# An encoder block with retention and windowed attention: attention's other work dealt out by K steps, values in a place of their own, sums and decays of the setup moved

## The chip, the cores and the metric

The kernel runs on one core of a Trainium2 chip. The metric is the device time of one execution in microseconds (us), and of several executions the median is taken. All engines of the core (TensorE for matmuls, VectorE, ScalarE, GpSimd, and SyncE, which issues transfers) run at the same time and wait for each other by semaphores. A row of the profile names them PE (with PEld for the load of weights into it), DVE, ACT, POOL and SP.

## The reference

One layer of a bidirectional encoder over 1024 positions and 16 learned meta tokens, with a width of 1024, in 32-bit floating point:

```python
u = _rms_norm(h, pre_w)
z = u @ w_in                      # q, k, v, gates of both branches
...
o_r = _bidirectional_retention(rq, rk, rv, lg_f, lg_b)[:, META_PAD:]   # 4 heads, decays exp(i * log_sigmoid(dec))
...
y_r = o_r.astype(h.dtype) @ w_rb
...
o_a = _windowed_sink_attention(aq, ak, av, sink)[:, META_PAD:].reshape(B, T, ATT_Q)   # 8 heads, 2 groups
o_a = o_a * jax.nn.silu(ag.astype(jnp.float32))
y_a = o_a.astype(h.dtype) @ w_ab
mix = jax.nn.sigmoid(gr) * y_r + jax.nn.sigmoid(ga) * y_a
out = mix @ w_o
return h + _rms_norm(out, post_w)
```

Retention is computed in chunks of 128 positions, forward and backward with decays of their own. Attention takes blocks of 128 queries against the block before, the same block, the block after and the 16 meta keys.

## The kernel before

**Numbers in two parts.** Each 32-bit operand is given to TensorE as two operands of the type fp32r: a high part (a copy into that type, by ScalarE or, in `pool_hi`, by GpSimd) and a low part (operand minus high part, by VectorE in `dve_lo`, L77). A product is three matmuls, high by high, low by high and high by low (`mm3`, L69 to L71). One step over 128 of the 1024 input channels is called a K step; a whole projection of a tile, `proj`, has eight K steps, 24 matmuls.

**Setup (to about 42 us).** `x` comes in eight slices `xr0` to `xr7`. For each, ScalarE makes the high part and VectorE the low part (L317), TensorE runs one K step of retention's first query and key projections for all tiles (`qk0_mm`), ScalarE squares the slice, and a running sum of squares is kept (`add_square`, L306; the first sum is on GpSimd, the others on VectorE). The weights of the first query and key come in parts (`w0_part`). The decays are a chain of small operations on VectorE (`decays`, `decay_series`, `decay_exponents`, L192 to L211), with powers on GpSimd (L214, L269). After that `pack_meta` copies the meta columns into `xm` (L128, four casts), the first values' weights `wv0` are split (one low half on VectorE, L77, one on GpSimd, L102), and the projections `pv0_0`, `pv0_1` and so on follow. The rope rotation of a projection (`rope_evac`, L161 to L164) is three operations of VectorE that read the PSUM bank, and an addition on GpSimd.

**Retention (to about 347 us).** Four heads; beside each head's scans a generator supplies projections of the next. `fill()` takes the next item of a generator, here one whole projection. At the end of a head the output is normalized (L584), transposed (L552) and scaled (L557), and stored to DRAM by SyncE.

**Attention (about 347 to 597 us).** Four head pairs of eight query blocks. For a block, `stage1` splits the query (GpSimd L74, VectorE L77), makes the scores of both heads in the two PSUM banks of `p2`, adds the mask and takes the row maximum on VectorE (L1202), takes the exponential on ScalarE (L1204), and scales on GpSimd (L1216). `stage2` transposes the result (L1226 to L1233) and splits it again (`pah`, `pal`, `pbh`, `pbl`). `stage3` multiplies it with the values. The values are projected by `gen_av` (nine groups, `pav`) into `vraw`, which lies in the pool `ap`; that pool opens when retention's pool is closed. Beside `gen_av` runs `sums_of_x`: SyncE loads slices of x again (L661), ScalarE scales them (L666), VectorE takes four differences of each (L668), and SyncE stores them (L672). `FILL_A` names the blocks after which a projection is traced: of the same head pair's second half, of the next head pair, in head pair 2 of the second group of keys, and in head pair 3 of gates 6 and 5 (`gen_gate`).

**Output (to the end).** Blocked matrix products of both branches and of the output, one long run of matmuls.

**What sets the order.** Each engine works in an order that is fixed when the kernel is built. A scheduler with a model of the time picks it: what is traced earlier has priority, and what waits can be overtaken by something else that is ready. `tc.issue_after(p)` pins: what is traced inside stands behind instruction `p` in the order. Buffers of a tag, and PSUM banks (three `pj`, two `p1`, two `p2`, one `p3`), are given out in turn.

Of the kernel before, what the change touches and what calls it, by code (L numbers as in the profile page):

```python
# [14 lines left out]
NM = 16  # L15
# [10 lines left out]
FILL_A = (0, 1, 3, 4, 5, 6)  # L26
# [12 lines left out]
def block_kernel(ctx: ExitStack, tc: tile.TileContext, xT, x, w_in, w_rb, w_ab, w_out, vecs, dec, sink,  # L39
# [50 lines left out]
    def load_w(src, u, act=False):  # L90
        hi, lo = [], []
        for s in range(2):
# [8 lines left out]
            if act and s:  # L101
                nc.gpsimd.tensor_tensor(l, raw, h.bitcast(F32), ALU.subtract)  # L102
            else:
                dve_lo(l, raw, h)
# [84 lines left out]
    def decays():  # L189
# [6 lines left out]
        return v.tensor_scalar(acc, ss, 1.0 / 17, None, op0=ALU.mult).ins  # L196
# [20 lines left out]

    def decay_table(hs):
        for h in hs:
# [3 lines left out]
            nc.scalar.activation(t, t, AF.Exp)  # L223
            nc.vector.tensor_scalar(DT[:, h], t, SCALE, None, op0=ALU.mult)
# [17 lines left out]
    with tc.tile_pool(name="setup", bufs=1, reuse_waits="tile") as st:  # L242
# [24 lines left out]
        exponentials()  # L267
        with tc.issue_after(raised[0]):
            nc.gpsimd.tensor_tensor(e, ecst[:, 0:8], na, ALU.pow)  # L269
# [18 lines left out]
        for i in range(6):  # L288
# [16 lines left out]
        def add_square(k):  # L305
            sums[k] = (nc.vector if k > 1 else nc.gpsimd).tensor_tensor(squares[k], squares[k - 1], squares[k], ALU.add).ins  # L306

        for k in range(KT):
            t = xr[k]
            if k == 1:  # L310
                with tc.issue_after(head):
                    series = decays()
            parts = [(0, 528), (528, T)] if k == 0 else [(0, T)]
            for a, b in parts:
                nc.scalar.activation(xh[k][:, a:b], t[:, a:b], AF.Copy, scale=vec[:, k:k + 1])
                with tc.issue_after(sums[k - 2]) if k > 3 else tc.issue_after(series) if k == 1 else ExitStack():
                    low = nc.vector.scalar_tensor_tensor(xl[k][:, a:b], t[:, a:b], vec[:, k:k + 1],  # L317
                                                         xh[k][:, a:b].bitcast(F32), op0=ALU.mult, op1=ALU.subtract)
                if not a:
                    head = low.ins  # L320
            if k == 1:
# [4 lines left out]
                decay_columns()  # L326
            if k == 3:
                fifth()
# [3 lines left out]
            if k > 1:  # L332
                with tc.issue_after(low.ins), tc.issue_after(exponents):
# [19 lines left out]
        with tc.issue_after(split):  # L353
            evac_qk0(0)
# [53 lines left out]

    r_stack = ExitStack()
    rp = r_stack.enter_context(tc.tile_pool(name="rp", bufs=1, reuse_waits="tile"))  # L410

    def gen_qk(h):
# [3 lines left out]
        for i, (a, b) in enumerate(PIECES):  # L416
            t = proj(w, P, a, b, f"pk{h}_{i}")
            rope_evac(t, a, b, kt[:, i], f"k{h}_{i}")
            yield
        for i, (a, b) in enumerate(HALVES):  # L420
            t = proj(w, 0, a, b, f"pq{h}_{i}")
# [7 lines left out]
    def retention(h, fill):  # L429
# [133 lines left out]
        for c in range(NB, 0, -1):  # L563
# [54 lines left out]
    def gen_aq(hp, i):  # L618
# [4 lines left out]
        for e_ in range(2):  # L623
            t = proj(wq[hp], P * e_, a, b, f"paq{hp}_{i}{e_}")
# [8 lines left out]
    def gen_ak(g):  # L633
# [4 lines left out]
        for i, (a, b) in enumerate(PIECES):  # L638
            t = proj(wak[0], P * g, a, b, f"pak{g}_{i}")
# [777 lines left out]
```

## Time and profile before

| | us |
|---|---|
| median of 3 runs (lowest, highest) | 1098.11 (1097.82, 1101.93) |
| the profiled execution's own time | 1098.95 |
| its span, first to last instruction | 1097.2 |
| around the span | 1.75 |
| TensorE busy | 1072.2 (98%) |
| VectorE busy | 877.4 (80%) |
| ScalarE busy | 488.4 (45%) |
| GpSimd busy | 247.9 (23%) |
| mean granted clock of TensorE | 0.99 |

The profile shows one execution. Rows of a timeline give the start, the length, the engine, the line, the operation, what is written and read, the shapes, and how many in a row; in square brackets stands how long the engine had been idle before and what ended that. Grouped rows end with the busy time of the group, the mean of one in nanoseconds, and the idle time before them. The granted clock is the share of TensorE's full clock that the throttle allowed.

### The profile page before, as it was taken

The numbers are of one execution on the slowest core, as the hardware profiler recorded it, in microseconds if no ns is written. First come the engines' busy times: TensorE is split into PE (matmuls) and PEld (weight loads), VectorE is DVE, ScalarE is ACT, GpSimd is POOL, SyncE is SP. The second block draws the span as 40 slices with busy tenths as digits, with TensorE's granted clock in tenths as the row PEclk, the third lists the DMA queues.
The fourth block names the chain that finished last, engine by engine and source line by source line (L and its number), as shares of the span: only waits on it lengthen the run. The fifth ranks groups of instructions, "written<-read, shape, count | busy, mean of one in ns | idle before, by whom it ended". The sixth has DMA issues, their size and how long they took to land.

```text
span 1097.2 us, 17244 instructions
## 1 busy us (share of the span) xinstructions
PE 1072.2 (98%) x5973; PEld 925.4 (84%) x5973; DVE 877.4 (80%) x1868; ACT 488.4 (45%) x1132; POOL 247.9 (23%) x350
## 2 busy tenths in 40 slices
PE   8899999999998999999999999999999999999996
PEld 7899999998988988988887878888888788787885
DVE  7887778877957888988667876888889889867765
ACT  7141432513414454445667544454456446433442
POOL 5434324233322434455220000000000000110032
PEclk9899999998999999999999999999999999999999
DMA  7121111111115961121114763779874755789463
GB/s 287 39 77 38 42 40 58 59 40 39 59 40 183 321 225 49 40 77 58 50 49 154 251 208 124 247 229 349 275 272 129 228 199 199 233 201 330 121 115 78
DMA packets 75800, 159.46 MB, mean 145 GB/s; under 512 B 8128, under 2 KB 19904, under 8 KB 74944
## 3 DMA queue, kind: packets, MB, share of 16 engines
q1 hardware_dynamic: 71824, 151.78, 40.2%
q0 software_dynamic: 3456, 6.29, 3.8%
q8 instruction: 47, 0.77, 0.3%
q14 instruction: 41, 0.34, 0.1%
q10 hardware_dynamic: 432, 0.28, 0.1%
HBM read 105.89 MB, written 52.43 MB: 144 GB/s over the span
## 4 chain that ended last, share of the span: by engine, by line
PE 88%; DMA 5%; DVE 4%; ACT 1%; issue 1%; SPq 0%; POOL 0%; DVEq 0%; POOLq 0%; ACTq 0%
PE bz L70 6%; PE bz L69 6%; PE bz L71 6%; PE pv L69 3%; PE pv L70 3%; PE pv L71 3%; PE paq L70 3%; PE paq L71 3%; PE paq L69 3%; PE br L70 2%; PE bo L70 2%; PE bo L69 2%; PE bo L71 2%; PE br L69 2%; PE br L71 2%; PE ba L70 2%
## 5 line engine op out<-in xcount | busy, mean ns | idle before, releaser
L1051 POOL DMA_DIRECT2D mx_d<-c1a x4 | 3.7, 922 | 398.3 <-DVE c1a L1042 398.3
L70 PE MATMUL bz<-big,llz 128*128 128x512 f32 x208 | 82.4, 396 | 0.4 <-DVE llz L77 0.4
L71 PE MATMUL bz<-big,lhz 128*128 128x512 f32 x208 | 81.7, 394 | 0.0
L69 PE MATMUL bz<-big,lhz 128*128 128x512 f32 x208 | 81.2, 396 | 0.3 <-ACT lhz L772 0.3
L69 PE MATMUL pv<-wh,big 128*128 128x256 f32 x256 | 74.5, 291 | 0.0
L70 PE MATMUL pv<-wh,big 128*128 128x256 f32 x256 | 73.6, 287 | 0.0
L71 PE MATMUL pv<-wl,big 128*128 128x256 f32 x256 | 73.6, 287 | 0.0
L69 PE MATMUL bz<-T,lhz 128*128 128x512 f32 x156 | 61.7, 395 | 0.0
L70 PE MATMUL bz<-T,llz 128*128 128x512 f32 x156 | 61.5, 395 | 0.0
L71 PE MATMUL bz<-T,lhz 128*128 128x512 f32 x156 | 61.3, 394 | 0.0
L1204 ACT ACTIVATE p<-p,nm 128x400 f32<-128x400 f32 (+1 forms) x64 | 38.5, 602 | 35.3 <-DVE nm L1202 32.5
L1216 POOL TENSOR_SCALAR p<-p,den 128x400 f32<-128x400 f32 (+1 forms) x60 | 36.1, 612 | 71.0 <-DVE den L1210 44.5
L70 PE MATMUL paq<-big,wl 128*128 128x512 f32 x128 | 51.2, 400 | 0.0
L69 PE MATMUL paq<-big,wh 128*128 128x512 f32 x128 | 51.0, 398 | 0.0
L71 PE MATMUL paq<-big,wh 128*128 128x512 f32 x128 | 50.9, 397 | 0.0
L69 PEld LDWEIGHTS pv<-wh,big 128*128 128x128 f32 x256 | 49.5, 193 | 0.6 <-DVE vl L77 0.4
L70 PEld LDWEIGHTS pv<-wh,big 128*128 128x128 f32 x256 | 49.5, 193 | 0.1
L71 PEld LDWEIGHTS pv<-wl,big 128*128 128x128 f32 x256 | 49.3, 193 | 0.0
L77 DVE TENSOR_TENSOR wl<-wr,wh 128x1024 fp32r<-128x1024 f32 x33 | 46.1, 1400 | 3.2 <-POOL wh L74 3.1
L69 PEld LDWEIGHTS bz<-big,lhz 128*128 128x128 f32 x208 | 39.0, 188 | 10.4 <-ACT lhz L772 1.3
L70 PEld LDWEIGHTS bz<-big,llz 128*128 128x128 f32 x208 | 39.1, 188 | 9.7 <-DVE llz L77 0.6
L71 PEld LDWEIGHTS bz<-big,lhz 128*128 128x128 f32 x208 | 39.1, 188 | 9.0
(618 smaller groups left out, 3666.4 us busy)
## 6 DMA issues: line engine op xcount, KB each, us to landing
wr<-in_w_in_dram SPq DMA_DIRECT2D x35, 512.0 KB, 3.6
wrz<-in_w_in_dram SPq DMA_DIRECT2D x28, 512.0 KB, 5.4
tg<-tg_d SPq DMA_DIRECT2D x32, 256.0 KB, 4.9
T<-preT SPq DMA_DIRECT2D x6, 1024.0 KB, 8.0
oTr_d<-ost SPq DMA_DIRECT2D x16, 256.0 KB, 2.1
xs<-in_xT_dram SPq DMA_DIRECT2D x16, 256.0 KB, 5.0
xsT<-xs SPq DMA_DIRECT2D x16, 256.0 KB, 5.3
oTa_d<-oa SPq DMA_DIRECT2D x16, 256.0 KB, 2.2
```

Of the source, the lines that this page charges most:

```text
L69: nc.tensor.matmul(o, ah, bh, start=first, stop=False, **kw)
L70: nc.tensor.matmul(o, al, bh, start=False, stop=False, **kw)
L71: return nc.tensor.matmul(o, ah, bl, start=False, stop=last, **kw).ins
L77: return nc.vector.tensor_tensor(o, i, hi.bitcast(F32), ALU.subtract).ins
L1051: nc.gpsimd.dma_start(d, to, accum_op=ALU.add)
L1204: nc.scalar.activation(p[:, 0:wid], p[:, 0:wid], AF.Exp, scale=-1.0, bias=nm_[:, e_:e_ + 1], accum_out=den[:, e_:e_ + 1])
L1216: nc.gpsimd.tensor_scalar(pt[e_][:, 0:wid], pt[e_][:, 0:wid], den[:, e_:e_ + 1], 1.0, op0=ALU.mult, op1=ALU.mult)
```

## The change

The tables for dealing out work, and the generators: `proj` gives the control back after each K step but the last, so an item of a generator is now one K step (three matmuls). Retention asks for `fill(KT)`, eight of them. In attention the number of K steps after each block comes from `FILL`, and they stand behind the transposes of the block before (`turned[-2]`), or behind the last score. Gate 6 is taken out of head pair 3 and goes, two projections each, to head pairs 0 and 1.

```diff
-FILL_A = (0, 1, 3, 4, 5, 6)
+FILL = ((6,) * 8, (6,) * 8, (6, 6, 4, 4, 3, 3, 3, 3), (7, 7, 7, 7, 7, 6, 7))
...
@@ proj
             mm3(t[:, 0:b - a], wh(k, m0, m0 + P), wl(k, m0, m0 + P), xh[k][:, a:b], xl[k][:, a:b],
-                k == 0, k == KT - 1)
+                k == 0, k == KT - 1, True)
+            if k < KT - 1:
+                yield
...
@@ gen_qk, gen_aq, gen_ak, gen_gate
-            t = proj(wq[hp], P * e_, a, b, f"paq{hp}_{i}{e_}")
+            t = yield from proj(wq[hp], P * e_, a, b, f"paq{hp}_{i}{e_}")
...
@@ retention
-                    fill()
+                    fill(KT)
...
@@ attention
-    softmax = []
+    scored, softmax, turned = [], [], []
...
-                mm3(s[:, 0:wid], a_, b_, kh[:, start:start + wid], kl[:, start:start + wid], True, True)
+                scored.append(mm3(s[:, 0:wid], a_, b_, kh[:, start:start + wid], kl[:, start:start + wid], True, True))
...
-                nc.tensor.transpose(t2[0:NM, P * e_:P * e_ + P], pt[e_][:, moff:moff + NM], ident)
+                last_one = nc.tensor.transpose(t2[0:NM, P * e_:P * e_ + P], pt[e_][:, moff:moff + NM], ident).ins
...
+            turned.append(last_one)
...
             if n == NB - 2:
+                if hp == 3:
+                    with tc.issue_after(scored[-1]):
+                        fill(FILL[hp][n])
                 yield
             stage2(n)
-            if n in FILL_A:
-                fill(2 if hp == 3 else 1)
+
+            if hp < 3 or n < NB - 2:
+                with tc.issue_after(turned[-2] if len(turned) > 1 else scored[-1]):
+                    fill(FILL[hp][n])
...
+    gates6 = gen_gate(6)
+
+    def part(gen, n):
+        for _ in range(KT * n):
+            yield next(gen)
...
+        if hp < 2:
+            l.append(part(gates6, 2))
         if hp < 3:
             l.append(gen_aq(hp + 1, 0))
         else:
-            l += [gen_gate(6), gen_gate(5)]
+            l.append(gen_gate(5))
...
         if hp == 2:
-            fill(4)
+            fill(4 * KT)
```

The values' tiles `vraw`, `vm` and `vmt` leave the pool `ap` and get a pool of their own, which opens before retention's pool:

```diff
+    va_stack = ExitStack()
+    va = va_stack.enter_context(tc.tile_pool(name="va", bufs=1, reuse_waits="tile"))
+    vraw = va.tile([P, NB, 256], F32, name="vraw")
+    vm = va.tile([P, 256], R, name="vm")
+    vmt = va.tile([NM, 256], F32, name="vmt")
...
-    vraw = ap.tile([P, NB, 256], F32, name="vraw")
-    vm = ap.tile([P, 256], R, name="vm")
...
-            mt = None if c else ap.tile([NM, 256], F32, name="vmt")
+            mt = None if c else vmt
...
     a_stack.close()
+    va_stack.close()
```

In the setup the first sum of squares and the second low half of `wv0` go from GpSimd to VectorE; the decays' and indices' transfers are issued on ScalarE's queue behind its first exponential; the whole decay chain stands in one stretch behind the low part of slice 2, and what follows it on VectorE (low of slice 3, first sum, the fifth part of w0) is pinned behind its exponents; the exponents take fewer operations; the factor `SCALE` moves from the tables to the row factors `r2`; `wv0` is traced ahead of the last sum, and the first rope ahead of the split of the sum; the row sums go beside `pv0_2`; eight idle matmuls open the kernel instead of six.

```diff
@@ load_w
-            if act and s:
-                nc.gpsimd.tensor_tensor(l, raw, h.bitcast(F32), ALU.subtract)
-            else:
-                dve_lo(l, raw, h)
+            dve_lo(l, raw, h)
...
@@ decay_exponents
-        for o, base, j, n in ((0, 0, 0, 2), (4, 4, 1, 2), (16, 0, 4, 1)):
-            for i in range(n):
-                k = o + 8 * i
-                v.tensor_scalar(ex[:, k:k + 4], lg[:, base:base + 4], idx[:, j + 2 * i:j + 2 * i + 1], None, op0=ALU.mult)
+        v.tensor_tensor(ex[:, 0:16].rearrange("p (a b c) -> p a b c", a=2, b=2),
...
+        v.tensor_scalar(ex[:, 16:20], lg[:, 0:4], idx[:, 4:5], None, op0=ALU.mult)
...
-        for a, b in ((0, 8), (16, 20)):
-            nc.gpsimd.tensor_scalar(dtab[:, a:b], dtab[:, a:b], SCALE, 1.0, op0=ALU.mult, op1=ALU.mult)
...
-            nc.scalar.activation(t, t, AF.Exp)
-            nc.vector.tensor_scalar(DT[:, h], t, SCALE, None, op0=ALU.mult)
+            nc.scalar.activation(DT[:, h], t, AF.Exp)
...
-        nc.scalar.dma_start(dect, dec.partition_broadcast(P))
-        with tc.issue_after(nc.scalar.dma_start(idx, tab[:, MW + 3 * P:]).ins):
-            nc.scalar.activation(warm, warm, AF.Exp)
+        with tc.issue_after(nc.scalar.activation(warm, warm, AF.Exp).ins):
+            nc.scalar.dma_start(dect, dec.partition_broadcast(P))
+            nc.scalar.dma_start(idx, tab[:, MW + 3 * P:])
...
-        for i in range(6):
+        for i in range(8):
...
-            sums[k] = (nc.vector if k > 1 else nc.gpsimd).tensor_tensor(squares[k], squares[k - 1], squares[k], ALU.add).ins
+            sums[k] = nc.vector.tensor_tensor(squares[k], squares[k - 1], squares[k], ALU.add).ins
...
-                with tc.issue_after(sums[k - 2]) if k > 3 else tc.issue_after(series) if k == 1 else ExitStack():
+                with tc.issue_after(sums[k - 2] if k > 3 else exponents) if k > 2 else ExitStack():
...
-            if k == 1:
+            if k == 2:
                 with tc.issue_after(low.ins):
-                    third()
+                    decays()
                     decay_series()
                     exponents = decay_exponents()
                 decay_columns()
...
             if k == 3:
-                fifth()
+                with tc.issue_after(exponents):
+                    fifth()
...
-        add_square(KT - 1)
-        sq = squares[-1]
         with tc.issue_after(low.ins):
             pack_meta()
+            wv0 = load_w(w_in, U_V, act=True)
+
+        add_square(KT - 1)
         with tc.issue_after(sums[KT - 1]):
-            wv0 = load_w(w_in, U_V, act=True)
+            rotated = evac_qk0(0)
...
-        split = dve_lo(sql, sq, sqh)
+        with tc.issue_after(rotated):
+            split = dve_lo(sql, sq, sqh)
...
-        first = [projT(wv0, 0, "pv0_0", vmeta0), projT(wv0, 1, "pv0_1", None, sums_by_rows), projT(wv0, 2, "pv0_2")]
+        first = [projT(wv0, 0, "pv0_0", vmeta0), projT(wv0, 1, "pv0_1"), projT(wv0, 2, "pv0_2", None, sums_by_rows)]
...
         nc.vector.reciprocal(r2, ms)
-
+        nc.vector.tensor_scalar(r2, r2, SCALE, None, op0=ALU.mult)
```

More of the change, by code (lines that the diff above doesn't have):

```diff
@@ L195, in decays @@
         v.tensor_tensor(ss, s_, s_, ALU.mult)
-        return v.tensor_scalar(acc, ss, 1.0 / 17, None, op0=ALU.mult).ins
+        v.tensor_scalar(acc, ss, 1.0 / 17, None, op0=ALU.mult)
     def decay_series():
@@ L206, in decay_exponents @@
         v = nc.vector
[L207 to L210 removed]
+        v.tensor_tensor(ex[:, 0:16].rearrange("p (a b c) -> p a b c", a=2, b=2),
+                        lg.rearrange("p (b c) -> p b c", b=2).unsqueeze(1).to_broadcast([P, 2, 2, 4]),
+                        idx[:, 0:4].rearrange("p (a b) -> p a b", a=2).unsqueeze(3).to_broadcast([P, 2, 2, 4]), ALU.mult)
+        v.tensor_scalar(ex[:, 16:20], lg[:, 0:4], idx[:, 4:5], None, op0=ALU.mult)
         return v.tensor_scalar(ex[:, 20:28], lg, float(P), None, op0=ALU.mult).ins
@@ L305, in add_square @@
         def add_square(k):
-            sums[k] = (nc.vector if k > 1 else nc.gpsimd).tensor_tensor(squares[k], squares[k - 1], squares[k], ALU.add).ins
+            sums[k] = nc.vector.tensor_tensor(squares[k], squares[k - 1], squares[k], ALU.add).ins
         for k in range(KT):
             t = xr[k]
-            if k == 1:
-                with tc.issue_after(head):
-                    series = decays()
             parts = [(0, 528), (528, T)] if k == 0 else [(0, T)]
@@ L315, in block_kernel @@
                 nc.scalar.activation(xh[k][:, a:b], t[:, a:b], AF.Copy, scale=vec[:, k:k + 1])
-                with tc.issue_after(sums[k - 2]) if k > 3 else tc.issue_after(series) if k == 1 else ExitStack():
+                with tc.issue_after(sums[k - 2] if k > 3 else exponents) if k > 2 else ExitStack():
                     low = nc.vector.scalar_tensor_tensor(xl[k][:, a:b], t[:, a:b], vec[:, k:k + 1],
                                                          xh[k][:, a:b].bitcast(F32), op0=ALU.mult, op1=ALU.subtract)
-                if not a:
-                    head = low.ins
-            if k == 1:
+            if k == 2:
                 with tc.issue_after(low.ins):
-                    third()
+                    decays()
                     decay_series()
@@ L326, in block_kernel @@
                 decay_columns()
+            if k == 0:
+                with tc.issue_after(low.ins), tc.issue_after(raised[1]):
+                    exponentials()
+                    nc.gpsimd.tensor_tensor(e, ecst[:, 0:8], na, ALU.pow)
+            if k == 1:
+                third()
             if k == 3:
-                fifth()
+                with tc.issue_after(exponents):
+                    fifth()
             qk0_mm(k)
@@ L332, in block_kernel @@
             if k > 1:
-                with tc.issue_after(low.ins), tc.issue_after(exponents):
+                with tc.issue_after(exponents if k == 2 else low.ins):
                     add_square(k - 1)
-        add_square(KT - 1)
-        sq = squares[-1]
         with tc.issue_after(low.ins):
             pack_meta()
+            wv0 = load_w(w_in, U_V, act=True)
+        add_square(KT - 1)
         with tc.issue_after(sums[KT - 1]):
-            wv0 = load_w(w_in, U_V, act=True)
+            rotated = evac_qk0(0)
+        sq = squares[-1]
         sqh, sql = (st.tile([P, T], R, name=n) for n in ("sqh", "sql"))
         nc.scalar.copy(sqh, sq)
-        split = dve_lo(sql, sq, sqh)
+        with tc.issue_after(rotated):
+            split = dve_lo(sql, sq, sqh)
         pms = p1("pms")
@@ L416, in gen_qk @@
         for i, (a, b) in enumerate(PIECES):
-            t = proj(w, P, a, b, f"pk{h}_{i}")
+            t = yield from proj(w, P, a, b, f"pk{h}_{i}")
             rope_evac(t, a, b, kt[:, i], f"k{h}_{i}")
@@ L420, in gen_qk @@
         for i, (a, b) in enumerate(HALVES):
-            t = proj(w, 0, a, b, f"pq{h}_{i}")
+            t = yield from proj(w, 0, a, b, f"pq{h}_{i}")
             o = ra.tile([P, 512], F32, tag="q", bufs=6, name=f"qr{h}_{i}")
@@ L638, in gen_ak @@
         for i, (a, b) in enumerate(PIECES):
-            t = proj(wak[0], P * g, a, b, f"pak{g}_{i}")
+            t = yield from proj(wak[0], P * g, a, b, f"pak{g}_{i}")
             o = ra.tile([P, 272], F32, tag="ak", bufs=2, name=f"akr{g}_{i}")
@@ L702, in gen_gate @@
             for e_ in range(2):
-                t = proj(w, P * e_, a, b, f"pgt{u}_{a}{e_}")
+                t = yield from proj(w, P * e_, a, b, f"pgt{u}_{a}{e_}")
                 o = ra.tile([P, 512], F32, tag="m1", bufs=2, name=f"gt{u}_{a}{e_}")
```

4 lines of the change are left out of this document (removed).

## The prediction

> **What bounds the kernel now.** I read the busy times first, then the idle time of TensorE with what ended it, then a table by stage with the granted clock, and only then single rows.
>
> ```profile
> span 1097.2 us, 17244 instructions
> PE 1072.2 (98%) x5973; PEld 925.4 (84%) x5973; DVE 877.4 (80%) x1868; ACT 488.4 (45%) x1132; POOL 247.9 (23%) x350
> ```
>
> TensorE is busy for 1072.2 of 1097.2 us, and the change leaves its matmuls alone but for two idle ones at the start. So a gain can only come from its gaps and from the stretches at half clock, and a loss from new gaps. The waits of TensorE (for what, total, times, longest), and stretches by stage (length, busy time of PE, PEld, DVE, ACT, POOL, granted clock, DMA share, GB/s):
>
> ```profile
> PE pv L138 <- DVE wl L77: 3.4, 1, 3.4
> PE to L552 <- DVE op L584: 3.1, 3, 1.6
> ```
>
> ```profile
> 31.20:34.60 3.40, 1.36 (x8) 0.89 (x7) 3.40 (x6) 0.00 (x0) 0.90 (x1) 1.00 0.00 0
> 34.60:41.40 6.80, 5.35 (x27) 4.67 (x28) 6.64 (x12) 1.83 (x3) 1.50 (x2) 0.50 0.44 154
> 345.20:348.60 3.40, 1.95 (x10) 1.25 (x11) 2.40 (x8) 2.63 (x9) 1.17 (x4) 1.00 0.40 130
> 348.60:352.10 3.50, 3.50 (x19) 3.50 (x18) 1.47 (x5) 1.64 (x5) 0.00 (x0) 0.51 0.85 253
> 352.10:591.00 238.90, 238.90 (x1448) 212.86 (x1447) 189.90 (x495) 125.25 (x368) 93.48 (x151) 1.00 0.33 115
> 591.00:597.80 6.80, 5.24 (x26) 3.37 (x25) 6.28 (x13) 6.67 (x18) 0.00 (x0) 1.00 0.84 274
> 370.00:440.00 70.00, 70.00 (x398) 61.31 (x397) 62.98 (x153) 32.28 (x100) 32.54 (x49) 1.00 0.48 165
> ```
>
> The reader is to see three things. Two stretches lose time that this change touches: the setup (a wait of 3.4, then 6.8 at half clock) and the end of retention (PE 1.95 of 3.40, then 3.5 at half clock). Attention, 352.1 to 591.0, has no gap at all: 238.90 of 238.90 at clock 1.00. So dealing its other work more finely has nothing to win there but at the last 6.8 us, and can only lose. And VectorE is the engine behind it that has least room, 62.98 of 70.00 busy from 370 to 440.
>
> **Setup: sums, decays, order of the lows.**
>
> ```profile
> 11.24 2.61 POOL L306 TENSOR_TENSOR sq<-sq,sq 128x1040 f32<-128x1040 f32 x1 [0.88 <-ACT sq L331]
> 29.11 2.99 POOL L102 TENSOR_TENSOR wl<-wr,wh 128x1024 fp32r<-128x1024 f32 x1 [0.45 <-ACT wh L98]
> 11.44 2.43 DVE L201 SCALAR_TENSOR_TENSOR acc<-acc,ss 128x8 f32<-128x8 f32 x1
> 15.89 0.77 DVE L201 SCALAR_TENSOR_TENSOR acc<-acc,ss 128x8 f32<-128x8 f32 x4
> 20.07 1.23 DVE L306 TENSOR_TENSOR sq<-sq,sq 128x1040 f32<-128x1040 f32 x1
> 29.74 2.62 DVE L128 CAST xm<-big 128x64 fp32r<-128x64 f32 x3
> 33.43 0.18 DVE L128 CAST xm<-big 128x64 fp32r<-128x64 f32 x1
> 34.78 1.22 DVE L77 TENSOR_TENSOR wl<-wr,wh 128x1024 fp32r<-128x1024 f32 x1
> 39.23 0.41 PE L69 MATMUL pv<-wh,big 128*128 128x256 f32 x1
> ```
>
> Two long operations go from GpSimd to VectorE: the first sum, 2.61 there and 1.23 here, and a low half, 2.99 there and 1.22 here. VectorE pays 2.45 for them, and gets back what it lost beside them: 2.43 for an operation whose like takes 0.77/4 = 0.19, and 2.62 for three casts of 0.18, so 2.2 + 2.1 = 4.3. The Trainium skill, SBUF — State Buffer, section "Who interferes with whom", calls the port pair of VectorE and GpSimd an exclusive lock: whoever comes second stands until the other is done. Both rows agree, each as long as the rest of GpSimd's operation.
>
> The decays cost x3's low: seventeen small operations of about 0.19 (3.2 in all) now run in one stretch ahead of it, and TensorE waits 1.7 at about 20. Laid along the built order of the changed kernel, the last low of x ends 1.0 later than before, at 30.8; then three casts (0.3) and both value lows (2 x 1.22) end at 33.5 instead of 36.0. The fourth cast stands behind sum 6 (34.6), and the second values' projection waits until sum 7 and the first rope row have freed its bank, at 37.15. Before, it began at 39.23: 2.1 saved. From there to 41.4 the clock was halved; if it is not, 1.1 more. Term -3.2; ends: -1.0 if the clock halves there all the same, -4.6 if those two waits fall too (3.4 + 1.1). The transfers of decays and indices move on ACT's queue behind the table load; their exponents are needed ten microseconds later, so nothing. Fewer small operations on GpSimd, the factor folded into the row factors, the row sums' small matmuls in the next projection and two more idle matmuls ahead of the first operand: nothing, TensorE or GpSimd is idle there or does them either way.
>
> **Values' own place.**
>
> ```profile
> 345.25 0.41 PE L552 MATMUL to<-ident,op 128*128 128x128 f32 x2 [1.64 <-DVE op L584]
> 346.11 0.41 PE L552 MATMUL to<-ident,op 128*128 128x128 f32 x2 [0.44 <-DVE op L584]
> 346.96 0.65 PE L69 MATMUL ps<-kTh,aqh 128*128 128x272 f32 x2 [0.44 <-POOL aqh L74]
> 348.12 0.38 PE L69 MATMUL pav<-wh,big 128*128 128x256 f32 x1 [0.51 <-ACT vraw L1149]
> 352.23 0.28 PE L69 MATMUL pav<-wh,big 128*128 128x256 f32 x1
> 352.35 0.28 PE L70 MATMUL pav<-wh,big 128*128 128x256 f32 x1
> 347.67 5.89 SPq L661 DMA_DIRECT2D xs<-in_xT_dram  x11
> 353.81 4.33 DVE L668 TENSOR_TENSOR xs<-xs,xs 128x512 f32<-128x512 f32 x6 [0.59 <-ACT xs L666]
> 367.00 2.06 DVE L77 TENSOR_TENSOR wl<-wr,wh 128x1024 fp32r<-128x1024 f32 x1
> 370.51 1.21 DVE L77 TENSOR_TENSOR wl<-wr,wh 128x1024 fp32r<-128x1024 f32 x1
> ```
>
> With `vraw` outside `ap`, values' projections need not wait until retention's tiles are released, and they fill its tail: 1.64 + 0.44 + 0.44 + 0.51 = 3.0 idle, and half of 3.5 at clock 0.51 (1.75). Term -4.8; at least -3.0, if the clock stays.
>
> But they were the cover of the next stage. Before, the first scores stood ahead of six value groups; in the built order all nine groups stand ahead of them. TensorE is through at 348.12 - 3.2 - 3.0 + 144 x 0.118 (the step between the two pav rows) = 358.9, and the second block's scores need the two banks that VectorE's mask-adds of the first must free. These stand behind seven sums of x and gate 6's first low half. Loads for those sums leave behind the last stores of retention, whose transposes stay behind value groups on TensorE, so they keep their time (347.67), and the seven subtractions end at 353.81 + 4.33 = 358.1. The low half adds 1.21 to 2.06; two halves split by GpSimd beside the subtractions may add 0.85 each (2.06 - 1.21). Mask-adds (0.49) then end between 359.8 and 362.3, so TensorE waits 0.9 to 3.4, and 0.8 more in the same place if the next query low falls behind the second half. I take 4.0, near the top, because an eighth subtraction stands there too, and half a window of clock (1.7), because 1.95 busy of 3.40 was enough for that at 345.2. Term +5.7; ends 0 and +7.6 (4.2 and two windows). On the clock the Trainium skill, TensorE: Matmul & The Clock Gate, Part 1, says the clock halves after an idle window of about 3.4 us. This trace halves it after windows 40% and 57% busy, so the measurement goes further; read to the letter, the page would spare the 1.7.
>
> **Steps of three matmuls, pinned.**
>
> ```profile
> L1202 DVE CUSTOM_DVE_ANT_0 p<-ps,mask,nsink 128x272 f32<-128x272 f32 x14 | 6.4, 493 | 0.7 <-PE pt L1233 0.7
> L1204 ACT ACTIVATE p<-p,nm 128x272 f32<-128x272 f32 x14 | 7.2, 518 | 5.5 <-DVE nm L1202 5.5
> L1204 ACT ACTIVATION_READ_ACCUMULATOR p<-p,nm 128x1 f32 x55 | 10.3, 188 | 0.0
> L77 DVE TENSOR_TENSOR aql<-aq,aqh 128x128 fp32r<-128x128 f32 x55 | 19.6, 376 | 11.2 <-POOL aqh L74 11.0
> L1216 POOL TENSOR_SCALAR p<-p,den 128x272 f32<-128x272 f32 x14 | 6.7, 491 | 17.3 <-DVE den L1210 10.4 <-ACT gt L706 4.8 <-ACT pm L1240 1.1
> L77 DVE TENSOR_TENSOR wl<-wr,wh 128x1024 fp32r<-128x1024 f32 x11 | 15.9, 1448 | 0.0
> L161 DVE TENSOR_TENSOR m_aq<-paq,cr 128x512 f32<-128x512 f32 x14 | 9.5, 681 | 0.1
> L77 DVE TENSOR_TENSOR pbl<-pt,pbh 128x256 fp32r<-128x256 f32 x18 | 7.6, 421 | 3.3 <-ACT pbh L1248 3.1
> 430.71 0.35 PE L69 MATMUL ps<-kTh,aqh 128*128 128x400 f32 x1
> 430.90 0.35 PE L70 MATMUL ps<-kTh,aql 128*128 128x400 f32 x1
> ```
>
> Nothing is computed more or less; the pins say where it may stand. At the start of head pairs 1, 2 and 3 the built order has the scores of blocks 0, 1 and 2 back to back and no projection until block 0's transposes. Block 0's chain after its last score: mask-add 0.49, exponential 0.52 and 0.19, two scalings on GpSimd 0.98, so 2.2 alone. VectorE, in order, has the next block's two mask-adds (0.98 at least) and two query lows (0.75) between: 3.9. TensorE has four scores of three matmuls of 0.19 to do, 2.2 (the step between the two rows of ps). The wait is 1.7, three times, and in head pair 2 part of a weight half (0.9 of 1.45) stands ahead too: +6.0; ends 0 (the chain alone, 2.2, is just covered) and 9, with the weight half in all three and the denominators' small operations.
>
> In block 1 of head pairs 0, 1 and 2, `pbl` stands on VectorE behind the rope of a projection just ended (3 x 0.68) and a weight half (1.45). With itself 0.42 that is 3.9, against 0.8 of transposes and output matmuls on TensorE: 3.1 in head pair 0. In 1 and 2 the rope starts earlier by the built order and leaves 0.9 and 1.9. Together +5.9; ends 0, if the scheduled neighbours run early, and 9.3 for three alike.
>
> Gate 6's two weight loads come forward on SP's queue, ahead of retention's last stores, where transfers take 0.40 of the engines (345.2): nothing. Its four projections leave head pair 3, whose last stretch then holds the softmax chain with less beside it. Of 6.80 - 5.24 = 1.56 idle I take 1.2 off; ends 0 and -1.6.
>
> **Sum.** -3.2 - 4.8 + 5.7 + 6.0 + 5.9 - 1.2 = +8.4, on the profiled execution's 1098.95: 1107.35. That execution is 0.84 over the median 1098.11, so for the median 1106.5.
>
> **Rivals.** (a) Faster: VectorE gets to block 0's mask-adds before TensorE has finished the values, and the chains run as early elsewhere. This decides at one place: if the seventh subtraction ends by 357 instead of 358.1 and the low half stays at 1.21, the entry wait is gone. With all waits in attention gone, 1098.1 - 9.2 = 1088.9. For it: the present order shows no gap in 238.9 us with the same work. Against: VectorE is 90% busy from 370, and the cover is what moved.
> (b) No change: the entry (5.7) and head pair 0's `pbl` (3.1) stay, the rest hides: 1098.1 - 9.2 + 8.8 = 1097.7. For it: the remaining waits are 0.9 to 2.0, within what a few operations on VectorE in another order change.
> (c) The clock: other waits of 2 to 3 us fall into single windows and halve the next one, 1.7 each: two more give 1109.9, all six of them 1116.7. For it: 1.95 busy of 3.40 sufficed; against: 5.24 of 6.80 at the end of attention did not.
>
> **How the numbers follow.** Forecast with its own range 1103 to 1112: 0.58. (a) 0.16, (b) 0.16, (c) beyond 1109: 0.10. The measurement can tell about 0.5%, 5.5 us, from no change: below 1092.6 is faster, above 1103.6 slower. So faster 0.16, same 0.16, slower 0.68. The range 1092 to 1113 leaves out most of (a) and the far part of (c), about 0.18.
>
> **What would show it.** Right: value matmuls at 340 to 350 at full clock, a gap on TensorE at about 359 that ends with a mask-add (VectorE, `nm` or `p`), gaps before the first transposes of head pairs 1 to 3 at about 435, 507 and 560, and one at 390 that ends with `pbl`; the value low at 33.5 and the second value projection near 37. Wrong: the stretch from 352 to 591 still full on PE, or the sums of x ending before the values do. Wrong in size: half clock in the table by stage at other places than 359.

## The result and the profile after

The changed kernel took 1107.74 us in the median of six runs (1105.55 to 1110.61), the kernel before 1098.07 (six runs, 1097.82 to 1101.93). The ratio is 1.0084, with a 95% interval of 1.0063 to 1.0104: slower by 9.7 us, where 8.4 were forecast (1106.5). The execution that was profiled is the longest of the six, 1110.61, so the trace shows 11.7 more than that of before.

The page of the kernel after, and what its TensorE waited for (total, times, longest):

```profile
span 1108.8 us, 17219 instructions
PE 1075.4 (97%) x5975; PEld 925.3 (83%) x5975; DVE 869.3 (78%) x1864; ACT 489.6 (44%) x1132; POOL 240.1 (22%) x346
```

```profile
PE ps L69 <- DVE nm L1204: 5.1, 6, 3.3
PE po L71 <- DVE pbl L77: 5.1, 3, 3.0
...
PE pt L1228 <- POOL p L1218: 1.5, 3, 0.6
...
PE pv L69 <- DVE m_qk L162: 1.2, 1, 1.2
```

The two waits of before (3.4 for a low half of the value weights, 3.1 for the normalized output) are gone from the head of this list. In their place stand two of 5.1, both in attention, both on VectorE. By stage (length, busy time of PE, PEld, DVE, ACT, POOL, granted clock, DMA share, GB/s), kernel after:

```profile
36.80:40.30 3.50, 3.50 (x18) 3.50 (x19) 3.44 (x6) 0.40 (x1) 1.11 (x2) 0.51 0.02 9
345.20:352.10 6.90, 6.90 (x61) 6.90 (x60) 1.50 (x7) 4.04 (x12) 0.00 (x0) 1.00 0.54 164
357.70:361.10 3.40, 0.62 (x5) 0.40 (x4) 3.30 (x5) 2.33 (x4) 2.83 (x3) 1.00 1.05 402
361.10:367.90 6.80, 6.26 (x15) 4.96 (x16) 6.75 (x21) 2.86 (x10) 0.83 (x2) 0.50 1.02 358
385.00:388.40 3.40, 0.39 (x3) 0.19 (x3) 3.31 (x6) 0.58 (x1) 1.85 (x1) 1.00 0.76 230
388.40:391.80 3.40, 3.40 (x12) 2.79 (x13) 2.90 (x10) 1.91 (x6) 2.65 (x6) 0.50 1.00 388
352.10:601.00 248.90, 236.49 (x1353) 204.99 (x1352) 185.38 (x493) 126.30 (x367) 93.78 (x151) 0.98 0.31 104
```

The tail of retention is full now and at full clock (6.90 of 6.90 at 1.00). Attention, which was full, is not: 236.49 of 248.90, and two long holes, at 357.7 and at 385.0, are each followed by half clock. The rows of the first hole, TensorE and then VectorE:

```profile
358.04 0.29 PE L71 MATMUL ps<-kTl,aqh 128*128 128x272 f32 x1
361.64 0.67 PE L69 MATMUL ps<-kTh,aqh 128*128 128x400 f32 x1 [3.31 <-DVE nm L1204]
```

```profile
353.39 2.22 DVE L672 TENSOR_TENSOR xs<-xs,xs 128x512 f32<-128x512 f32 x3 [0.28 <-ACT xs L670]
356.24 2.90 DVE L672 TENSOR_TENSOR xs<-xs,xs 128x512 f32<-128x512 f32 x2 [0.64 <-ACT xs L670]
359.07 1.30 DVE L77 TENSOR_TENSOR wl<-wr,wh 128x1024 fp32r<-128x1024 f32 x1
360.30 0.77 DVE L672 TENSOR_TENSOR xs<-xs,xs 128x512 f32<-128x512 f32 x1
360.99 0.49 DVE L1204 CUSTOM_DVE_ANT_0 p<-ps,mask,nsink 128x272 f32<-128x272 f32 x1
```

TensorE ends the first block's scores at 358 and starts the second block's at 361.64. In between VectorE works off differences of x and the first low half of gate 6's weights, and only then comes the mask-add. Two of the differences take 1.45 each instead of 0.7; GpSimd makes the high halves of gate 6's weights at that time (from 356.12 and from 357.54, about 1.05 each). The second hole, TensorE and then VectorE:

```profile
384.95 0.28 PE L70 MATMUL po<-pbh,vl 128*128 128x256 f32 x1
388.23 0.45 PE L71 MATMUL po<-pbl,vh 128*128 128x256 f32 x1 [3.01 <-DVE pbl L77]
```

```profile
385.08 0.68 DVE L161 TENSOR_TENSOR m_aq<-paq,sr 64x512 f32<-64x512 f32 x1
385.77 0.69 DVE L162 TENSOR_TENSOR m_aq<-paq,sr 64x512 f32<-64x512 f32 x1
386.50 1.23 DVE L77 TENSOR_TENSOR wl<-wr,wh 128x1024 fp32r<-128x1024 f32 x1
387.75 0.42 DVE L77 TENSOR_TENSOR pbl<-pt,pbh 128x256 fp32r<-128x256 f32 x1
```

The low part that TensorE waits for takes 0.42. It comes 3 late because the three operations of a rope (the first of them starts at 384.38) and a weight half, here of head pair 1's queries, stand ahead of it.

The trace confirms the places that were forecast. Whether the causes are the ones that were named, it cannot tell: the kernel has three edits at once.

### The profile page after: what moved, and what is told of

The parts are those of the page before. It is cut to its first block, busy times and chain, and to the rows that moved or that the text cites. A ratio compares the mean times of both kernels' runs of the same rounds, so it can differ in the third digit from the quotient of the medians.

```text
span 1108.8 us, 17219 instructions
## 1 busy us (share of the span) xinstructions
PE 1075.4 (97%) x5975; PEld 925.3 (83%) x5975; DVE 869.3 (78%) x1864; ACT 489.6 (44%) x1132; POOL 240.1 (22%) x346
## 4 chain that ended last, share of the span: by engine, by line
PE 85%; DVE 6%; DMA 4%; issue 2%; ACT 1%; POOL 1%; SPq 0%; DVEq 0%; POOLq 0%; ACTq 0%
PE bz L70 7%; PE bz L71 7%; PE bz L69 7%; PE pv L69 3%; PE pv L70 3%; PE pv L71 3%; PE bo L70 2%; PE br L70 2%; PE bo L69 2%; PE bo L71 2%; PE br L69 2%; PE br L71 2%; PE ba L70 2%; PE ba L71 2%; PE ba L69 2%
```

## The experiments

Times are medians; each ratio is to the kernel before, run on the same chip in the same job. Tiles keep their names in all kernels; line numbers shift by a few.

### Each part alone, and the change without the dealing

`deal_undone`: setup and the values' place as after; the tables, `yield`s, pins and gate 6 as before.

```diff
-FILL = ((6,) * 8, (6,) * 8, (6, 6, 4, 4, 3, 3, 3, 3), (7, 7, 7, 7, 7, 6, 7))
+FILL_A = (0, 1, 3, 4, 5, 6)
...
-            if hp < 3 or n < NB - 2:
-                with tc.issue_after(turned[-2] if len(turned) > 1 else scored[-1]):
-                    fill(FILL[hp][n])
+            if n in FILL_A:
+                fill(2 if hp == 3 else 1)
```

> The change without the dealing: setup and values' place as after, attention's other work as before (whole projections, no pins, gate 6 in head pair 3). Theory of the prediction: -3.2 - 4.8 + 5.7 = -2.3, 1095.8, with the entry wait at 359. Rival: no wait at 359; -8.0, less what the scheduler gives back in its new order of attention (waits of 1 to 3 at 380 and at the end of attention): 1091 to 1097.

Measured: 1094.68, ratio 0.9961 (0.9944 to 0.9979).

`deal_alone`: the kernel before with the dealing and nothing else.

```diff
-FILL_A = (0, 1, 3, 4, 5, 6)
+FILL = ((6,) * 8, (6,) * 8, (6, 6, 4, 4, 3, 3, 3, 3), (7, 7, 7, 7, 7, 6, 7))
...
-            if n in FILL_A:
-                fill(2 if hp == 3 else 1)
+            if hp < 3 or n < NB - 2:
+                with tc.issue_after(turned[-2] if len(turned) > 1 else scored[-1]):
+                    fill(FILL[hp][n])
```

> The kernel before, with the dealing alone (tables, steps, pins, gate 6 split), the setup and the values' place as before. Theory of the prediction: starts of head pairs +6.0, pbl +5.9, end -1.2, no entry wait, because six value groups are again between the first scores and the next: 1098.1 + 10.7 = 1108.8. Rival (pins alone make the entry wait): a wait of 3 to 5 at about 368 to 373 too, behind the value groups, and half a window of clock: 1098.1 + 15 = 1113.

Measured: 1113.16, ratio 1.0132 (1.0100 to 1.0164). First the table by stage of `deal_undone`, then two rows of TensorE in `deal_alone`:

```profile
359.00:366.00 7.00, 7.00 (x33) 5.81 (x33) 7.00 (x16) 2.87 (x8) 2.02 (x3) 1.00 0.98 342
584.00:598.00 14.00, 11.02 (x58) 8.23 (x57) 13.20 (x29) 12.08 (x30) 0.00 (x0) 1.00 0.56 210
```

```profile
371.21 0.42 PE L69 MATMUL ps<-kTh,aqh 128*128 128x400 f32 x1 [3.69 <-DVE nm L1204]
372.97 0.70 PE L70 MATMUL ps<-kTh,aql 128*128 128x400 f32 x1 [0.80 <-DVE aql L77]
```

This decides against the prediction's account of the entry wait. With the values in their own place and no dealing there is no hole at the entry at all: 7.00 of 7.00 busy. (Its end of attention, the second row, is idle for 3.0; before, it was 1.6.) With the dealing and the values in their old place the hole is there in full, 3.69 and 0.80, only ten microseconds later. So the hole belongs to the dealing and not to the values' place, and the time of `deal_alone` is the rival's 1113, not the prediction's 1108.8.

`values_alone`: the kernel before with the pool `va` alone.

```diff
+    va = va_stack.enter_context(tc.tile_pool(name="va", bufs=1, reuse_waits="tile"))
+    vraw = va.tile([P, NB, 256], F32, name="vraw")
...
-    vraw = ap.tile([P, NB, 256], F32, name="vraw")
```

> The kernel before with the values' place alone. Prediction: the tail of retention gains 4.8, and the entry wait costs 5.7 at about 362 to 367: +0.9, 1099.4, with a gap on TensorE there. Rival: the tail gains 4.8 and there is no entry wait, since projections of head pair 0 fill TensorE until VectorE is there; some of it is lost to other waits (2 near 384, 1 to 2 at the end of attention): 1095 to 1099, with PE full from 352 to 380.

Measured: 1100.55, ratio 1.0023 (1.0006 to 1.0040).

```profile
340.00:352.00 12.00, 12.00 (x104) 11.98 (x103) 6.20 (x21) 5.97 (x20) 2.61 (x6) 1.00 0.14 48
352.00:385.00 33.00, 32.77 (x192) 28.70 (x190) 27.08 (x50) 16.52 (x35) 15.67 (x15) 1.00 0.86 295
584.00:600.00 16.00, 13.66 (x74) 11.09 (x72) 14.32 (x36) 14.10 (x38) 0.30 (x1) 0.83 0.76 247
```

The tail is full and there is no entry hole, as the rival said. The time is nevertheless 1.5 above the top of its range. Its profiled execution, 1102.76, is near the top of ten (1096.06 to 1103.13) and 3.8 over that of before, though the tail gained 4.8. About 4 more than before are lost at the end of attention, where 13.66 of 16.00 are busy at a mean clock of 0.83 (12.44 of 14.00 at 1.00 before); 1.7 goes in retention, which nobody edited, where the clock is halved from 195.35 to 198.75; and 0.8 in two waits near 386. The profile does not place the rest.

`setup_alone`: the kernel before with the setup's edits alone.

```diff
-            sums[k] = (nc.vector if k > 1 else nc.gpsimd).tensor_tensor(squares[k], squares[k - 1], squares[k], ALU.add).ins
+            sums[k] = nc.vector.tensor_tensor(squares[k], squares[k - 1], squares[k], ALU.add).ins
...
         with tc.issue_after(low.ins):
             pack_meta()
+            wv0 = load_w(w_in, U_V, act=True)
```

The other lines of the change up to the row factors `r2` are in it too.

> The kernel before with the setup's edits alone. Prediction: second values' projection near 37 instead of 39.2, no half clock from 34.6 to 41.4, -3.2. So 1098.5 - 3.2 = 1095.3. Rival: the setup gains as said, but the scheduler, free to choose, lays the end of attention otherwise and gives it back there in waits of 0.6 to 2.0 on the softmax chain (587 to 596, about 3 more than before, and half a window or two of clock): 1098 to 1101.

Measured: 1099.38, ratio 1.0021 (1.0008 to 1.0034). Its end of attention, and that of before:

```profile
584.00:598.00 14.00, 10.92 (x51) 8.50 (x50) 12.25 (x29) 11.32 (x31) 0.00 (x0) 0.76 0.42 130
```

```profile
584.00:598.00 14.00, 12.44 (x73) 9.86 (x72) 9.30 (x22) 10.58 (x27) 0.00 (x0) 1.00 0.77 263
```

The setup's gain is there (its second value projection starts at 35.8, before 39.2), and it is given back 550 us later, where nothing was edited: 1.5 less busy, and the clock at 0.76. The order of attention is another one there (51 matmuls against 73 in the same 14 us). Alone, then, neither of the two parts gains anything; together, without the dealing, they gain 0.4%.

### The pins

`no_pins`: the change as it is, but nothing inside attention is pinned.

```diff
             if hp < 3 or n < NB - 2:
-                with tc.issue_after(turned[-2] if len(turned) > 1 else scored[-1]):
-                    fill(FILL[hp][n])
+                fill(FILL[hp][n])
```

The other pin, behind the last score in head pair 3, is taken off in the same way.

> The change without the two pins around fill in attention (tables, steps of three matmuls, values' place and setup all stay). Theory of the prediction: the entry wait at about 359 comes from the values' place and stays (3.5 on TensorE and half a window of clock, 5.7); the waits at the starts of head pairs 1 to 3 and before pbl come from the pins and go (11.9). Time: 1107.7 - 11.9 = about 1096, with a gap at 359 that ends with a mask-add. Rival: all waits of attention, the entry too, come from the pins, and go; then the stretch 352 to 590 is full on PE and nothing waits at 359; the softmax chain at the end of attention, no longer dealt work by hand, may wait again as it did before the change (2 to 4). Time: 1098.1 - 3.2 - 4.8 + 0 to 5 = 1090 to 1095.

Measured: 1096.72, ratio 0.9975 (0.9958 to 0.9992). The two pins cost some 11 us: 1107.7 with them and 1096.7 without.

```profile
359.00:366.00 7.00, 7.00 (x33) 5.81 (x32) 7.00 (x16) 3.25 (x9) 2.01 (x3) 1.00 0.97 347
583.10:586.50 3.40, 1.36 (x10) 0.95 (x8) 3.34 (x12) 3.09 (x9) 0.00 (x0) 1.00 1.03 390
586.50:593.40 6.90, 5.75 (x22) 4.50 (x23) 5.74 (x12) 5.42 (x15) 0.00 (x0) 0.51 0.12 44
```

No hole at the entry, where projections of head pair 0 (`paq`) now follow the first scores from 358.11, and none before `pbl`. What remains is the end of attention, where the last blocks wait for their own chain and the clock drops. In time the prediction's theory (1096) did as well as the rival (1090 to 1095); in the trace only the rival holds, and the end of attention eats the difference.

`no_first_pin`: only the first block of head pair 0 loses its pin.

```diff
-                with tc.issue_after(turned[-2] if len(turned) > 1 else scored[-1]):
+                with tc.issue_after(turned[-2]) if len(turned) > 1 else ExitStack():
```

> The change without the pin of the very first block alone (head pair 0, block 0 is no longer behind the last score). If the entry wait is the values' place: it stays 3.5 and the time 1107.7. If it is the pin: projections of block 0 fill TensorE while VectorE is at the sums of x, the wait of 3.3 at 359 to 362 goes or is spread over smaller ones of 0.4 to 2.3 further on (362 to 370), and the time is 2 to 5 below, 1103 to 1106. All waits from 385 on stay in both.

Measured: 1106.08, ratio 1.0066 (1.0044 to 1.0087). The hole does not vanish. It moves to the next pinned place: in its trace TensorE waits 2.3 at 366 for the next mask-add and 0.9 at 368 for a scaling, instead of 3.3 at 361.6. A single pin less gains only 1.7, and the intervals of the two ratios overlap (the change: 1.0063 to 1.0104).

### What the waits are made of

`no_sums`: the change without 12 of the 16 differences of x.

```diff
-            for n, o, a, b in SUMS:
+            for n, o, a, b in SUMS[:4 * (k // 3)]:
                 nc.vector.tensor_tensor(x[k, *o], x[k, *a], x[k, *b], ALU.subtract)
```

> The change with 12 of the 16 differences of sums_of_x left out (those of k = 0, 1, 2; ScalarE's scaling, loads and stores stay, so wrong data are stored). If the queue of VectorE ahead of the first mask-adds makes the entry wait, as the prediction worked it out (seven or eight differences of 0.69): the wait of 3.3 at 359 to 362 falls to about 1, the rest being the low halves of gate 6's weights. Waits from 385 on stay or grow, since VectorE's order shifts. Time 2 to 4 below the change's, 1104 to 1106. If transfers or ScalarE make it: the wait stays at 3 or more.

Measured: 1108.55, ratio 1.0115 (1.0085 to 1.0144). The waits of TensorE in its trace:

```profile
357.03 0.42 PE L69 MATMUL ps<-kTh,aqh 128*128 128x400 f32 x1 [0.67 <-DVE nm L1204]
359.06 0.45 PE L70 MATMUL ps<-kTh,aql 128*128 128x400 f32 x1 [0.92 <-DVE aql L77]
```

```profile
378.45 0.39 PE L71 MATMUL po<-pal,vh 128*128 128x256 f32 x1 [1.21 <-DVE pal L77]
384.11 0.58 PE L71 MATMUL po<-pbl,vh 128*128 128x256 f32 x1 [3.88 <-DVE pbl L77]
```

VectorE's queue makes the entry wait: with the differences gone it falls from 3.31 to 0.67. The expected gain in time did not come. Waits further on grew, from none to 1.21 and from 3.01 to 3.88 (the weight half ahead of `pbl` took 2.32 there in place of 1.23), the clock was halved from 382.5 to 389.3, and the whole, in two runs, is no faster. In this pinned order, time saved at one pin was waited for at the next.

`gate_6_back`: gate 6's projections go back to head pair 3, the pins stay.

```diff
-FILL = ((6,) * 8, (6,) * 8, (6, 6, 4, 4, 3, 3, 3, 3), (7, 7, 7, 7, 7, 6, 7))
+FILL = ((6, 6, 4, 4, 3, 3, 3, 3), (6, 6, 4, 4, 3, 3, 3, 3), (6, 6, 4, 4, 3, 3, 3, 3), (12, 12, 12, 11, 11, 11, 11))
...
-        if hp < 2:
-            l.append(part(gates6, 2))
...
-            l.append(gen_gate(5))
+            l += [gates6, gen_gate(5)]
```

> The change with gate 6's four projections back in head pair 3 (tables (6, 6, 4, 4, 3, 3, 3, 3) for head pairs 0 to 2, (12, 12, 12, 11, 11, 11, 11) for 3), pins kept. If gate 6's weights, split on VectorE at the entry, make the entry wait: it falls by 1.2 to 2.7 and the time with it, 1104 to 1106. If the sums of x and the pins make it: the entry wait stays, the waits before pbl grow (less work to hide them in head pairs 0 and 1), 1109 to 1113.

Measured: 1112.56, ratio 1.0137 (1.0114 to 1.0159). The entry wait stays to the digit, and the wait for `pbl` grows from 5.1 to 6.4:

```profile
PE po L71 <- DVE pbl L77: 6.4, 4, 3.0
PE ps L69 <- DVE nm L1204: 4.8, 5, 3.3
```

So gate 6 in particular is not the cause. The run does not clear weight halves as such: two still stand at the entry on VectorE (1.31 from 356.13, ahead of the mask-adds, and 1.21 from 358.89), which by the kernel are now those of the next weights loaded, head pair 1's queries. In `no_sums` a weight half stands there too (1.22 from 355.24), and TensorE waits 0.67 without the differences; so the differences are the larger part. With its own tables this kernel is slower than the change, and moving gate 6 forward seems to help a little by giving TensorE more to do in head pairs 0 and 1; that was not tested apart.

`table_9_3`: in head pairs 0 and 1, block 2 gets nine K steps and block 3 three. The projection that ends in block 2 still ends after its fourth K step there; three more K steps then follow on TensorE before `pbl` is needed.

```diff
-FILL = ((6,) * 8, (6,) * 8, (6, 6, 4, 4, 3, 3, 3, 3), (7, 7, 7, 7, 7, 6, 7))
+FILL = ((6, 6, 9, 3, 6, 6, 6, 6), (6, 6, 9, 3, 6, 6, 6, 6), (6, 6, 4, 4, 3, 3, 3, 3), (7, 7, 7, 7, 7, 6, 7))
```

> The change with the third and fourth entry of the tables of head pairs 0 and 1 at 9 and 3 instead of 6 and 6: the projection that ends in block 2 is no longer the one whose rope stands ahead of pbl. If the rope of a just ended projection holds pbl: in head pair 0 the wait before it goes from 3.0 to about 1.5 and the half clock after it goes, in head pair 1 the wait of 0.7 goes, head pair 2 (unchanged table) keeps 1.7, and the time is 3 to 5 below, 1103 to 1105. If pbl waits for something else (the transposes, ScalarE's copy): nothing moves, 1107.7.

Measured: 1103.56, ratio 1.0056 (1.0035 to 1.0076).

```profile
PE po L71 <- DVE pbl L77: 2.6, 2, 1.6
```

```profile
383.05 1.23 DVE L77 TENSOR_TENSOR wl<-wr,wh 128x1024 fp32r<-128x1024 f32 x1
384.78 0.38 PE L71 MATMUL po<-pbl,vh 128*128 128x256 f32 x1 [1.07 <-DVE pbl L77]
384.40:387.80 3.40, 3.02 (x16) 2.62 (x17) 3.15 (x10) 1.25 (x4) 3.15 (x6) 1.00 1.02 400
```

The three waits for `pbl` become two and 5.1 becomes 2.6, the clock stays at 1.00 behind the place, and the medians fall by 4.2 (ratio 1.0084 to 1.0056, 3.1; their intervals overlap). The queue ahead of `pbl` has not changed: the rope of a projection that has just ended (380.93 to 383.01) and a weight half still stand directly ahead of it on VectorE, as the prediction worked it out. What changed is the cover. Three K steps of about 0.7 each stand on TensorE behind the end of the projection, and they hide 1.9 of the 3.0.

`pins_whole`: whole projections behind the same pins.

```diff
-FILL = ((6,) * 8, (6,) * 8, (6, 6, 4, 4, 3, 3, 3, 3), (7, 7, 7, 7, 7, 6, 7))
+FILL = ((8, 8, 0, 8, 8, 8, 8, 0), (8, 8, 0, 8, 8, 8, 8, 0), (8, 8, 0, 8, 8, 0, 0, 0), (8, 8, 8, 8, 8, 8, 0))
```

> The change with tables in multiples of eight, so that whole projections stand behind the same pins ((8, 8, 0, 8, 8, 8, 8, 0) for head pairs 0 and 1, (8, 8, 0, 8, 8, 0, 0, 0) and (8, 8, 8, 8, 8, 8, 0) for 2 and 3). If steps of three matmuls cost the time themselves: no slower than the change, 1108 or less. If the pins cost it and the small steps soften that: blocks with nothing to do wait 2 to 4 more in head pairs 0 and 2 (at 388, 441, 526, 555), with half clock behind some: 1115 to 1123.

Measured: 1125.08, ratio 1.0251 (1.0221 to 1.0281).

```profile
PE ps L69 <- DVE nm L1204: 15.6, 6, 5.0
```

The time is 2 above the range expected for the pins. The small steps are not the loss. Behind pins they save some 17 us against whole projections, whose table leaves some blocks with nothing; without pins, whole projections (`deal_undone`, 1094.7) do no worse than steps (`no_pins`, 1096.7).

### A version that beats both

`late_pins`: pins are kept in head pair 3 from block 3 on, where work runs out, and nowhere else.

```diff
             if hp < 3 or n < NB - 2:
-                with tc.issue_after(turned[-2] if len(turned) > 1 else scored[-1]):
+                with tc.issue_after(turned[-2]) if hp == 3 and n > 2 else ExitStack():
                     fill(FILL[hp][n])
```

The pin behind the last score in head pair 3 is off here too.

> The change with the pin kept in head pair 3 from block 3 on only, where the work runs out. If the pins cost where VectorE is full and help where other work is short: no waits at 359, 390, 433, 505, as without pins, and the waits at the end of attention (1.1 + 1.9 + 1.2 + 0.4 without pins, with the clock halved for 6.8) go too, against small ones of 0.4 to 1.0 at the start of head pair 3. Time: 1096.7 - 4.6 - 3.4 + 3 = about 1092, faster than both kernels. If the end of attention waits for its own chain whatever stands beside it: 1096.7.

Measured: 1091.84 (1087.15 to 1092.28), ratio 0.9939 (0.9917 to 0.9960).

```profile
352.10:585.00 232.90, 230.04 (x1350) 202.10 (x1349) 187.66 (x494) 125.53 (x369) 94.29 (x151) 1.00 0.33 110
575.00:585.00 10.00, 9.63 (x53) 7.90 (x52) 4.94 (x14) 5.77 (x15) 0.00 (x0) 1.00 0.41 113
```

In the profiled execution attention is nearly full, its end too, and the clock never drops in it. That execution is the fastest of the five, by 3.5, with a mean clock of 0.998 against 0.994 to 0.996 in the others; where those lose it no trace shows. By the medians it is 16 us faster than the change and 6 faster than before.

## Why the prediction was right, and where it was not

The direction, the size and the range held: +8.4 forecast, +9.7 measured. Step by step:

**Setup, -3.2.** The steps hold. On VectorE and on TensorE, in the kernel after:

```profile
30.53 2.37 DVE L77 TENSOR_TENSOR wl<-wr,wh 128x1024 fp32r<-128x1024 f32 x2
```

```profile
36.63 0.43 PE L69 MATMUL pv<-wh,big 128*128 128x256 f32 x1 [1.23 <-DVE m_qk L162]
```

Both value lows end at 32.9 (33.5 forecast), and the second value projection starts at 36.63 (37.15), behind the three operations of the first rope. The wait for the low of x3 appears as said (1.4 at 19.56). The clock was the open end, and it fell on the bad side in the profiled execution: 0.51 from 36.8. A fixed mark far behind the setup shows what that is worth. The second transposes of retention's last head start, in before, after and `deal_undone`, at:

```profile
262.94 0.33 PE L463 MATMUL tr<-ident,kr 128*128 128x128 f32 x1 [0.61 <-ACT ost L557]
```

```profile
260.86 0.33 PE L467 MATMUL tr<-ident,kr 128*128 128x128 f32 x1 [0.61 <-ACT ost L561]
```

```profile
259.33 0.44 PE L465 MATMUL tr<-ident,kr 128*128 128x128 f32 x1 [0.61 <-ACT ost L559]
```

So -2.1 with the half clock and -3.6 without it; -3.2 lies between.

**Values' place, -4.8 at the tail.** Held: 6.90 of 6.90 at full clock.

**The entry, +5.7.** Its place, its arithmetic on VectorE and its size held: a wait of 3.3, and 6.8 at half clock, of which 6.26 were busy, so 3.1 lost, together 6.4. The cause that was named did not. The step that failed is "they were the cover of the next stage": the values' projections are not the only cover. Without pins the scheduler puts projections of head pair 0 into that place (`no_pins`, from 358.11); it is the pin behind the last score that forbids it. The forecast laid durations along the built order of the whole change, and that order was right; it put a price on a part without the built order of that part. With it, +5.7 belongs to the dealing and the three parts come to: dealing about +13 (1107.7 against 1094.7 without it; +14.5 alone), the two others together -4.

**Starts of head pairs, +6.0.** They are at the three places forecast, with the releasers forecast, but smaller. The list of waits gives 1.8 for mask-adds beside the entry's 3.3, 1.5 for the scalings on GpSimd and, in head pair 2, 0.4 for a query low: 3.7 idle where 6.0 was taken. The term was mis-sized.

**`pbl`, +5.9.** Measured 5.1, and 1.7 at half clock behind the longest, which the sum had left to a rival. The rows of VectorE show the queue that was forecast, and `table_9_3` that more work on TensorE behind the projection covers it.

**The end, -1.2.** The waits of the softmax chain went: before, TensorE waited 0.57, 0.21 and 0.29 at 592 to 596 for ScalarE, and in the kernel after there is none of these. In their place it waits 0.89 at 610 for a high part on ScalarE (`lhz`, an operand of the output stage), so little of the 1.2 is left. `late_pins` against `no_pins` has a fuller end (575 to 600: 24.63 busy against 20.84) and is about 4 us faster (0.9975 to 0.9939, intervals that just touch).

Taken together, -2.1 - 4.8 + 6.4 + 3.7 + 6.8 = +10.0, against 11.7 between the two profiled executions. The remaining 1.7 is not placed.

**The rivals.** (a) was wrong for the kernel as changed. Without pins its waits in attention do go, but not its time: 1096.7, not 1088.9, because the end of attention then loses more. The 238.9 us without a gap were the scheduler's doing, and "the same work shows no gap" was evidence for the freedom, not against the pins. (b) did not come. Of (c), one further half window came, behind 385.

## What to carry to other kernels

Where a scheduler sets each engine's order, a pin takes away its freedom to fill a hole; a pin belongs only where it would otherwise run out of work, and here the same pins cost 11 us everywhere and seem to gain about 4 in the last head pair. Price a part by the built order of that part, not of the whole: two parts can share one wait, and a part that gains alone at one place can be given back at another that nobody edited. When a small operation on an in-order engine is what the bottleneck waits for, read what stands ahead of it on that engine; shortening that queue at one place only moved the wait to the next pin.

## What was not expected of the hardware

Whether a half-empty stretch halves the clock varied between executions of the same instructions. In the kernel after and in `deal_undone` the setup is the same up to there. From 33.4 to 36.8 both were busy for 1.56 of 3.40; after it one got 0.51 and the other 1.00:

```profile
33.40:36.80 3.40, 1.56 (x12) 0.94 (x10) 3.34 (x7) 1.32 (x2) 0.14 (x1) 1.00 0.76 261
36.80:40.20 3.40, 3.40 (x17) 3.40 (x18) 3.34 (x6) 0.40 (x1) 1.01 (x2) 0.51 0.02 10
```

```profile
33.40:36.80 3.40, 1.56 (x12) 1.00 (x11) 3.34 (x7) 1.32 (x2) 0.22 (x1) 1.00 0.75 260
36.80:40.20 3.40, 3.40 (x30) 3.38 (x30) 3.34 (x6) 0.78 (x2) 1.02 (x2) 1.00 0.02 6
```

Longer holes (0.62 and 0.39 of 3.40 busy) were followed by half clock in the profile after. The Trainium skill, TensorE: Matmul & The Clock Gate, Part 1, describes windows of about 3.4 us that run freely; stretches of half clock of 3.4 and 6.8 agree with that, and so does an outcome that hangs on where a hole falls in its window. That the window must be idle does not agree: it was 46% busy here, as the profile counts, and in `values_alone` a stretch busy for 2.64 of 3.40 (from 191.95, with one wait of 0.61) stands right ahead of the half clock at 195.35. So the busy time of a stretch alone did not tell, in these traces, whether the clock would drop. The six runs of the change lie 5 us apart, and their mean clock goes from 0.991 in the longest to 0.995 in the shortest, which is the size of a few such windows.
